# Up projection with high and low activations in one 512-column operand; layer 0 started from a transposed x

## The chip, the core and the metric

The kernel runs on one core of a Trainium2 chip. Its engines, each with an instruction stream of its own: TensorE (PE, matmuls; PEld is its weight load), VectorE (DVE), ScalarE (ACT), GpSimd (POOL) and SyncE (SP, which here issues the transfers). Matmul results go to PSUM, all other tiles lie in SBUF. The metric is device time in microseconds (us), the median of several runs. Three runs of the kernel before gave 849.73, 849.77 and 851.79 us.

## The reference

Two decoder layers on 256 positions of 1024 channels, batch 1, all float32. In the names of the reference, a layer is:

```python
h = rmsnorm(x, norm_mix_pre)
proj = h @ w_in                       # 1024 -> 7168, split into the branches:
q, k, v, g_ret, sc_b, sc_c, sc_x, cf_a, cf_b, gate_logits = split(proj)
y_ret = (silu(g_ret) * head_groupnorm(retention(rotary(q), rotary(k), v))) @ w_ret_out
y_sc  = (sc_b * causal_dwconv(sc_c * sc_x, 3 taps)) @ w_sc_out
y_cf  = silu(layernorm(causal_dwconv(cf_a * sigmoid(cf_b), 31 taps))) @ w_cf_out
x = x + rmsnorm((sum of sigmoid(gate) * y over the three branches) @ w_o, norm_mix_post)
h = rmsnorm(x, norm_ffn_pre)
gate, val = split(causal_dwconv(h @ w_up, 3 taps))          # 1024 -> 2 x 2816
x = x + rmsnorm((silu(gate) * val) @ w_down, norm_ffn_post)
```

rmsnorm divides each row by the root of its mean square and multiplies by a gain per channel.

## The kernel before

**Precision.** Every matmul operand is held as a high part (rounded to TensorE's reduced float32 form) and a low part (what is left). A product takes three matmuls: high x high, high x low, low x high. The weights are split on the chip: ScalarE copies the raw unit into the high tile (L106), VectorE subtracts for the low tile (L107). Activations are split in the same way by `split` (L173 to L175).

**Weights.** All weights are packed on the host into units of 128 x 1024 float32 (512 KB), 142 per layer, in the order of their use. `Weights` (L66) loads a unit into one of four raw buffers (L79, on SP's queue), splits it into one of nine high/low pairs, and runs up to eight units ahead of the one in use (`pump`, L88). Units 0 to 11 of a layer and some later ones are split in two halves of 512 columns (`HALF`). A raw buffer can be loaded again once its low part is made.

**Two forms of projection.** In `xs_unit` (L304) the activation (128 channels by 128 positions) is stationary and 512 weight columns move: Q with K, V, the retention gate G, and the branch gates. `down_unit` (L315) does the same for the down and output projections. In `ws_block` (L270) the weights are stationary and 256 positions move, so that the result has channels on partitions, as the convolutions want: the conformer and short convolution projections, and the up projection. A block is one unit: for each of 8 slices of 128 channels a high-weight matmul with the high and one with the low activation (L274), then 8 low-weight matmuls (L277), all of 256 columns into the same half of a PSUM tile. `ws_pair` (L295) makes two blocks side by side in one tile. The operand `hT` is four tiles of (2 channel slices) x (high, low) x 256 positions.

**The start.** SP loads x of the first 128 rows, the identity, the gain (broadcast to all partitions), then weight units; x of the other 128 rows comes between. `prenorm` (L232) sums the squares on ScalarE, takes the power on GpSimd (L212) and multiplies on VectorE (L237). `to_hT` (L241) transposes on TensorE and splits into `hT`. Twelve matmuls on zeros (L200) run meanwhile. Layer 0 then computes Q and K for both row halves, with V between them, `rotary` (L349: four VectorE steps, four transposes, one copy), then the conformer projections (two B and two A pairs), then G, the short convolution, the branch gates and outputs, `w_o`, and the FFN.

**Background work.** Convolution taps, the retention steps and the layer norm are queued in `bgq` and taken off in slots with a budget (`bg`, L283) after projection blocks or units; what is left is forced before the outputs that need it.

**The up projection.** `up(i)` (L705) makes 256 gate and 256 value columns: the gate pair, `conv3` (L691: one ScalarE step and two VectorE taps per block, which read PSUM), Silu, the value pair, `conv3`, product, split. There are 11 pairs; the first two are computed by `fill` with stationary activations while the second norm finishes, and transposed afterwards by `fill_tr` (L754). From pair 3 on, the down matmuls of pair i - 3 follow each `up`. PSUM has eight tiles of 512 columns: four `mm` and four `ac`; in the up loop the `ac` tiles hold the down sums.

## Time and profile before

| what | value |
|---|---|
| median of three runs | 849.77 us (849.73 to 851.79) |
| the profiled execution's own time | 850.51 us |
| its span, first to last instruction | 848.7 us |
| mean granted TensorE clock | 0.994 |
| busy: PE, PEld, DVE, ACT, POOL | 833.5, 740.9, 655.4, 460.9, 17.9 us |
| moved by DMA | 157.02 MB, mean 185 GB/s |

The profile is of one execution. Its times are in microseconds from the start of the span. Rows of the time-ordered view give start and length, engine, line, operation, output<-input tiles, shapes, and in brackets the idle time of that engine before it with what ended the idleness. Rows of groups give line, engine, operation, tiles, shapes and count, then total busy time and the mean in ns, then the idle time before them. Matmuls are pipelined: the distance between the starts of two is what one costs, not its printed length.

### The profile page before, as it was taken

How to read it: one execution, taken by the hardware profiler on the slowest of the kernel's cores; microseconds unless marked ns; L12 is line 12 of the kernel's file. 1: busy time of each engine (PE TensorE's matmuls, PEld its weight loads, DVE VectorE, ACT ScalarE, POOL GpSimd, SP SyncE). 2: the span in 40 equal slices, each digit the busy share in tenths (PEclk: the TensorE clock that was granted, in tenths of full speed). 3: DMA queues.
4: the chain of work that ended last, by engine and by line, in shares of the span. 5: the costliest groups of instructions: out<-in, count | busy, mean ns of one | idle time of the engine just before them, and what ended most of it. 6: DMA issues, size and time to landing. Idle time of an engine off the chain costs nothing.

```text
span 848.7 us, 13172 instructions
## 1 busy us (share of the span) xinstructions
PE 833.5 (98%) x5036; PEld 740.9 (87%) x5036; DVE 655.4 (77%) x1086; ACT 460.9 (54%) x704; POOL 17.9 (2%) x28
## 2 busy tenths in 40 slices
PE   7999999999999999999999999999999999999997
PEld 4798988888879999999879899888887899999995
DVE  5889999775777976766695999996677698767652
ACT  5664464465666655455665435444666565555541
POOL 0000100000010000000010000000000000000000
PEclk8999999999999999999999999999999999999999
DMA  7885456655665565556566544566555555566511
GB/s 258 309 276 171 149 180 192 201 174 194 200 198 176 180 193 191 180 179 196 172 220 202 175 149 151 193 196 195 182 181 193 175 186 187 179 192 195 179 49 50
DMA packets 43695, 157.02 MB, mean 185 GB/s; under 512 B 4848, under 2 KB 5104, under 8 KB 43632
## 3 DMA queue, kind: packets, MB, share of 16 engines
q1 hardware_dynamic: 43632, 156.18, 57.2%
q8 instruction: 39, 0.64, 0.3%
q14 instruction: 24, 0.20, 0.1%
HBM read 155.12 MB, written 1.05 MB: 184 GB/s over the span
## 4 chain that ended last, share of the span: by engine, by line
PE 92%; DVE 2%; DMA 2%; issue 1%; ACT 1%; POOL 1%; SPq 0%; DVEq 0%; POOLq 0%; ACTq 0%
PE mm L274 25%; PE mm L277 13%; PE mm L309 8%; PE mm L311 8%; PE mm L310 8%; PE ac L320 5%; PE ac L322 5%; PE ac L324 5%; PE ac L311 4%; PE ac L309 4%; PE ac L310 4%; DMA raw<-w_dram 2%; DVE wlo L107 1%; PE mm L245 1%; POOL tn L212 1%
## 5 line engine op out<-in xcount | busy, mean ns | idle before, releaser
L106 ACT ACTIVATE whi<-raw 128x1024 fp32r<-128x1024 f32 (+1 forms) x320 | 296.5, 940 | 277.8 <-PE mm L274 109.2
L107 DVE TENSOR_TENSOR wlo<-raw,whi 128x1024 fp32r<-128x1024 f32 (+1 forms) x320 | 341.0, 1074 | 129.9 <-ACT whi L106 126.3
L274 PE MATMUL mm<-act,whi 128*128 128x256 f32 x1792 | 234.1, 283 | 0.0
L274 PEld LDWEIGHTS mm<-act,whi 128*128 128x128 f32 x1792 | 223.8, 191 | 2.2 <-ACT whi L106 0.7
L277 PE MATMUL mm<-act,wlo 128*128 128x256 f32 x896 | 125.8, 283 | 0.0
L277 PEld LDWEIGHTS mm<-act,wlo 128*128 128x128 f32 x896 | 115.6, 192 | 0.0
L309 PE MATMUL mm<-whi,act 128*128 128x512 f32 x288 | 113.0, 392 | 0.0
L311 PE MATMUL mm<-wlo,act 128*128 128x512 f32 x288 | 112.2, 390 | 0.0
L310 PE MATMUL mm<-whi,act 128*128 128x512 f32 x288 | 112.1, 389 | 0.0
L406 DVE SCALAR_TENSOR_TENSOR big<-big,par 128x229 f32<-128x229 f32 (+27 forms) x240 | 97.0, 462 | 0.0
L698 DVE SCALAR_TENSOR_TENSOR sm<-mm,par,sm 128x254 f32<-128x254 f32 (+1 forms) x176 | 72.7, 474 | 4.0 <-ACT sm L694 3.8
L320 PE MATMUL ac<-whi,act 128*128 128x512 f32 x228 | 71.3, 394 | 0.0
L324 PE MATMUL ac<-whi,act 128*128 128x512 f32 x228 | 70.6, 390 | 0.0
L322 PE MATMUL ac<-wlo,act 128*128 128x512 f32 x228 | 70.4, 390 | 0.0
L311 PEld LDWEIGHTS mm<-wlo,act 128*128 128x128 f32 x288 | 54.1, 188 | 11.4
L310 PEld LDWEIGHTS mm<-whi,act 128*128 128x128 f32 x288 | 54.1, 188 | 10.8
L309 PEld LDWEIGHTS mm<-whi,act 128*128 128x128 f32 x288 | 54.1, 188 | 10.9
L309 PE MATMUL ac<-whi,act 128*128 128x512 f32 x128 | 51.4, 402 | 0.8 <-ACT act L174 0.8
L322 PEld LDWEIGHTS ac<-wlo,act 128*128 128x128 f32 x228 | 42.8, 188 | 9.1
L324 PEld LDWEIGHTS ac<-whi,act 128*128 128x128 f32 x228 | 42.6, 188 | 9.2
L311 PE MATMUL ac<-wlo,act 128*128 128x512 f32 x128 | 50.5, 395 | 0.0
L310 PE MATMUL ac<-whi,act 128*128 128x512 f32 x128 | 50.3, 395 | 0.0
(104 smaller groups left out, 660.0 us busy)
## 6 DMA issues: line engine op xcount, KB each, us to landing
raw<-w_dram SPq DMA_DIRECT2D x284, 512.0 KB, 3.8
gain<-gain_dram SPq DMA_DIRECT2D x7, 512.0 KB, 5.0
xs<-x_dram SPq DMA_DIRECT2D x2, 256.0 KB, 3.2
gain<-gain_dram SPq DMA_DIRECT2D x2, 256.0 KB, 6.0
xs<-x_dram SPq DMA_DIRECT2D x1, 512.0 KB, 10.2
cs<-cst_dram SPq DMA_DIRECT2D x1, 512.0 KB, 6.9
out_dram<-xs SPq DMA_DIRECT2D x1, 512.0 KB, 2.6
out_dram<-xs SPq DMA_DIRECT2D x2, 256.0 KB, 2.0
```

What stands on the lines that cost most here:

```text
L106: self.nc.scalar.activation(out=hi[:, s], in_=r[:, s], func=AF.Copy)
L107: self.nc.vector.tensor_tensor(out=lo[:, s], in0=r[:, s], in1=hi[:, s].bitcast(F32), op=ALU.subtract)
L274: nc.tensor.matmul(o, wh[:, kt * P:(kt + 1) * P], rhs_h(hT, kt, hl), start=(kt == 0 and hl == 0), stop=False)
L277: nc.tensor.matmul(o, wl[:, kt * P:(kt + 1) * P], rhs_h(hT, kt, 0), start=False, stop=(kt == NKT - 1))
L309: nc.tensor.matmul(acc, lhs_h(hT, kt, 0, t), wh[:, s], start=(first and j == 0), stop=False)
L310: nc.tensor.matmul(acc, lhs_h(hT, kt, 1, t), wh[:, s], start=False, stop=False)
L311: nc.tensor.matmul(acc, lhs_h(hT, kt, 0, t), wl[:, s], start=False, stop=(last and j == 1))
L320: nc.tensor.matmul(acc[j], lh[:, tsl], hb(wh, j), start=first, stop=False)
L322: nc.tensor.matmul(acc[j], lh[:, tsl], hb(wl, j), start=False, stop=False)
L324: nc.tensor.matmul(acc[j], ll[:, tsl], hb(wh, j), start=False, stop=last)
L406: nc.vector.scalar_tensor_tensor(out=cc_t[:, b, sh:], in0=glu[:, b, :S - sh], scalar=tap, in1=cc_t[:, b, sh:], op0=ALU.mult, op1=ALU.add)
L698: nc.vector.scalar_tensor_tensor(out=dv[:, b, sh:], in0=pv[:, b, :S - sh], scalar=pp(PW_FF + (blk + b) * KS + 2 - sh), in1=dv[:, b, sh:], ...
```

## The change

Three things change.

In the up projection the high and the low activation of a channel slice, which lie next to each other, become one moving operand of 512 columns for the high weights (`ws_apart`). Products with the high activation land in the left half of a PSUM tile, those with the low one in the right half; the low-weight products, still of 256 columns, are added into the right half. Each block so takes a PSUM tile of its own, and `together` adds the two halves into an SBUF tile, one ScalarE copy and one VectorE add per block. `conv3` then reads SBUF. The transposes of the two filled pairs move to the `ac` tiles, and the value pair of pair 2 is computed ahead of the second filled pair.

Layer 0's Q, V and G are computed from x transposed on the host, times the gain, without the row norm; as the norm is a factor per row, it is applied to the results: in `rotary`, in v's copy, and in G's sigmoid and product. G moves ahead of the conformer projections, also in the order of the packed weights. The row factors are then spread over all partitions by two matmuls of ones with a diagonal, and the normalised operand for the later projections is made from the transposed x (`norm_xT`).

The first half of the first weight unit and the gain column are issued on ScalarE's queue, the first two units in halves; x in its usual form, the cosines and the identity are loaded after the first five units. The Sigmoid table is loaded before anything else on ScalarE's list of functions, and there are 9 warm-up matmuls for 12. The small tiles in SBUF (`sp`) have 10 buffers for 8.

The diff, cut to its core:

```diff
-WARM = 12
+WARM = 9
...
         while self.nd <= min(upto, self.n - 1):
             r = self.rpool.tile([P, 1024], F32, name="raw", tag="raw")
-            self.nc.sync.dma_start(out=r, in_=self.w[self.nd])
+            n = 512 if self.nd < 2 else 1024
+            for c in range(0, 1024, n):
+                eng = self.nc.scalar if self.nd == 0 and c == 0 else self.nc.sync
+                eng.dma_start(out=r[:, c:c + n], in_=self.w[self.nd][:, c:c + n])
             self.raw[self.nd] = r
...
-    sp = ctx.enter_context(tc.tile_pool(name="sp", bufs=8))
+    sp = ctx.enter_context(tc.tile_pool(name="sp", bufs=10))
...
-    nc.sync.dma_start(out=cs[:, :C_COS], in_=cst[:, :C_COS])
-    g_pre0 = gp.tile([P, D], F32, name="gain", tag="gain")
-    for j in range(2):
-        sl = slice(j * 512, (j + 1) * 512)
-        nc.sync.dma_start(out=g_pre0[:, sl], in_=gains[0, 0:1, sl].broadcast_to([P, 512]))
...
+    def load_xT(q):
+        a = xT[q // 2][:, 2 * (q % 2):2 * (q % 2) + 2, :]
+        nc.sync.dma_start(out=a, in_=xt[:, NKT + 512 * q:NKT + 512 * (q + 1)].rearrange("p (a b) -> p a b", b=S))
+
+    def split_xT(q):
+        for j in range(2):
+            kt = 2 * q + j
+            src = xT[kt // 4][:, kt % 4, :]
+            hi, lo = hT0[q][:, j, 0, :], hT0[q][:, j, 1, :]
+            nc.scalar.activation(out=hi, in_=src, func=AF.Identity, scale=gT[:, kt:kt + 1])
+            nc.vector.scalar_tensor_tensor(out=lo, in0=src, scalar=gT[:, kt:kt + 1],
+                                           in1=hi.bitcast(F32), op0=ALU.mult, op1=ALU.subtract)
+
+    load_xT(0)
+    nc.scalar.dma_start(out=gT, in_=xt[:, 0:NKT])
+    W.dma(0)
+    load_xT(1)
+    W.dma(1)
     nc.vector.memset(mhalf, -0.5)
+    ones = const.tile([P, P], F32, name="ones")
+    nc.vector.memset(ones, 1.0)
...
+    def ws_apart(hT, o):
+        i, wh, wl = W.get()
+        for kt in range(NKT):
+            nc.tensor.matmul(o, wh[:, kt * P:(kt + 1) * P],
+                             hT[kt // 2][:, kt % 2, :, :].rearrange("p a b -> p (a b)"),
+                             start=(kt == 0), stop=False)
+        for kt in range(NKT):
+            nc.tensor.matmul(o[:, S:2 * S], wl[:, kt * P:(kt + 1) * P], rhs_h(hT, kt, 0),
+                             start=False, stop=(kt == NKT - 1))
+        W.rel(i)
+
+    def ws_pair_apart(hT):
+        pt = [mm_t(), mm_t()]
+        for b in range(2):
+            ws_apart(hT, pt[b])
+        return pt
+
+    def together(pt):
+        a = sm_t()
+        for b in range(2):
+            ab = a[:, b * S:(b + 1) * S]
+            nc.scalar.activation(out=ab, in_=pt[b][:, S:2 * S], func=AF.Copy)
+            nc.vector.tensor_tensor(out=ab, in0=pt[b][:, 0:S], in1=ab, op=ALU.add)
+        return v2(a)
...
+            def times(out, in0, in1):
+                if rs is None:
+                    nc.vector.tensor_tensor(out=out, in0=in0, in1=in1, op=ALU.mult)
+                else:
+                    nc.vector.scalar_tensor_tensor(out=out, in0=in0, scalar=rs, in1=in1,
+                                                   op0=ALU.mult, op1=ALU.mult)
+
+            times(a.rearrange("p (h d) -> p h d", d=32), ps.rearrange("p (h d) -> p h d", d=32),
+                  cos[t].unsqueeze(1).broadcast_to([P, 16, 32]))
...
+        def ret_g(rs=None):
+            ga = [ac_t(), ac_t()]
+            for k in range(4):
+                u = get_xs(k)
+                for t in range(NT):
+                    xs_unit(u, hT if rs is None else hT0, ga[t], t, k == 0, k == 3)
+                W.rel(u[0])
+                if rs is None:
+                    bg(BG_CF)
+            for t in range(NT):
+                sg = sm_t()
+                if rs is None:
+                    nc.scalar.activation(out=sg, in_=ga[t], func=AF.Sigmoid)
+                    nc.vector.tensor_tensor(out=gs[:, t, :], in0=ga[t], in1=sg, op=ALU.mult)
+                else:
+                    nc.scalar.activation(out=sg, in_=ga[t], func=AF.Sigmoid, scale=rs[t])
+                    nc.vector.scalar_tensor_tensor(out=gs[:, t, :], in0=ga[t], scalar=rs[t], in1=sg,
+                                                   op0=ALU.mult, op1=ALU.mult)
+
...
+        if l == 0:
+            def both(k, acc):
+                u = get_xs(k)
+                for t in range(NT):
+                    xs_unit(u, hT0, acc[t], t, k == 0, k == 3)
+                W.rel(u[0])
+
+            for k in range(4):
+                both(k, qa)
+            rs = [rsq(sum_sq([hb(xs[:, t, :], 0), hb(xs[:, t, :], 1)])) for t in range(NT)]
+            dg = []
             for t in range(NT):
-                xs_unit(u, hT, va[t], t, False, k == 3)
-            W.rel(u[0])
-        for t in range(NT):
-            nc.scalar.activation(out=v_s[:, t, :], in_=va[t], func=AF.Copy)
+                dg.append(sm_t()[:, 0:P])
+                nc.vector.tensor_scalar(out=dg[t], in0=ident, scalar1=rs[t], scalar2=None,
+                                        op0=ALU.mult)
+            both(0, va)
+            rotary(0, qa[0], rs[0])
+            both(1, va)
+            rotary(1, qa[1], rs[1])
+            both(2, va)
+            rows = mm_t()
+            for t in range(NT):
+                nc.tensor.matmul(rows[:, t * P:(t + 1) * P], ones, dg[t], start=True, stop=True)
+            both(3, va)
+            for t in range(NT):
+                nc.scalar.activation(out=v_s[:, t, :], in_=va[t], func=AF.Identity, scale=rs[t])
+
+            def norm_xT(q):
+                xn = sm_t()
+                for j in range(2):
+                    kt = 2 * q + j
+                    nc.vector.scalar_tensor_tensor(out=v2(xn)[:, j, :], in0=xT[kt // 4][:, kt % 4, :],
+                                                   scalar=gT[:, kt:kt + 1], in1=rows[:, 0:S],
+                                                   op0=ALU.mult, op1=ALU.mult)
+                split(v2(xn), hT[q][:, :, 0, :], hT[q][:, :, 1, :])
+
+            for q in range(4):
+                norm_xT(q)
+            ret_g(rs)
+        else:
...
-        ga = [ac_t(), ac_t()]
-        for k in range(4):
-            u = get_xs(k)
-            for t in range(NT):
-                xs_unit(u, hT, ga[t], t, k == 0, k == 3)
-            W.rel(u[0])
-            bg(BG_CF)
-        for t in range(NT):
-            sg = sm_t()
-            nc.scalar.activation(out=sg, in_=ga[t], func=AF.Sigmoid)
-            nc.vector.tensor_tensor(out=gs[:, t, :], in0=ga[t], in1=sg, op=ALU.mult)
+        if l:
+            ret_g()
...
-            pv, dv = v2(ps), v2(dst)
+            pv, dv = ps, v2(dst)
...
-        def up(i, pg=None, pv=None):
-            pg = ws_pair(hT2) if pg is None else pg
+        def up(i, pg=None, pv=None, ga_ps=None):
+            pg = together(ws_pair_apart(hT2) if ga_ps is None else ga_ps) if pg is None else pg
             ga = sm_t()
             conv3(pg, ga, 2 * i)
             gsl = sm_t()
             nc.scalar.activation(out=gsl, in_=ga, func=AF.Silu)
-            pv = ws_pair(hT2) if pv is None else pv
+            pv = together(ws_pair_apart(hT2)) if pv is None else pv
...
         def fill_tr(i):
-            pgv = [mm_t(), mm_t()]
+            pgv = [ac_t(), ac_t()]
...
         up(0, *fill_tr(0))
-        g2 = ws_pair(hT2)
+        g2 = together(ws_pair_apart(hT2))
+        v2_ = together(ws_pair_apart(hT2))
         up(1, *fill_tr(1))
         acc = [[ac_t(), ac_t()] for _ in range(NT)]
         for i in range(NFILL, NPAIR):
-            up(i, *((g2,) if i == NFILL else ()))
+            up(i, *((g2, v2_) if i == NFILL else ()))
...
     hT = new_hT()
-    xg = prenorm(0, g_pre0)
-    to_hT(0, xg, hT)
-    W.pump(1)
-    nc.sync.dma_start(out=xs[:, 1, :], in_=x[P:S, :])
-    W.pump(3)
-    xg = prenorm(1, g_pre0)
-    nc.sync.dma_start(out=cs[:, C_COS:C_DEC], in_=cst[:, C_COS:C_DEC])
+    preload(AF.Sigmoid, mhalf[:, 0:1])
+    for q in range(4):
+        if q > 1:
+            load_xT(q)
+        split_xT(q)
+        W.pump(q)
+    nc.sync.dma_start(out=cs[:, :C_DEC], in_=cst[:, :C_DEC])
+    for t in range(NT):
+        nc.sync.dma_start(out=xs[:, t, :], in_=x[t * P:(t + 1) * P, :])
     W.pump(LOOK)
...
+    if l == 0:
+        xs(win, OFF_G)
     for j in range(2):
         ws(win, OFF_B + 256 * j)
         ws(win, OFF_A + 256 * j)
-    xs(win, OFF_G)
+    if l:
+        xs(win, OFF_G)
...
```

More of the change, by code (lines that the diff above doesn't have):

```diff
@@ L125, in block_kernel @@
 @with_exitstack
-def block_kernel(ctx: ExitStack, tc: tile.TileContext, x, w, gains, par, cst, out):
+def block_kernel(ctx: ExitStack, tc: tile.TileContext, x, xt, w, gains, par, cst, out):
     nc = tc.nc
@@ L347, in get_xs, with rotary @@
             return u
-        def rotary(t, ps):
+        def rotary(t, ps, rs=None):
             a = sm_t()
@@ L382, in layer @@
[L382 to L396 removed]
+        if l == 0:
[8 more added lines that the diff above has]
+            dg = []
+            for t in range(NT):
+                dg.append(sm_t()[:, 0:P])
[24 more added lines that the diff above has]
+        else:
+            uq = [get_xs(k) for k in range(2)]
+            for k in range(2):
+                xs_unit(uq[k], hT, qa[0], 0, k == 0, False)
+            uq += [get_xs(k) for k in range(2, 4)]
+            for k in range(2, 4):
+                xs_unit(uq[k], hT, qa[0], 0, False, k == 3)
+            uv = [get_xs(k) for k in range(2)]
+            for k in range(2):
+                if k == TR1:
+                    to_hT(1, xg1, hT)
+                xs_unit(uv[k], hT, va[0], 0, k == 0, False)
+            for k in range(4):
+                xs_unit(uq[k], hT, qa[1], 1, k == 0, k == 3)
+                W.rel(uq[k][0])
+            rotary(0, qa[0])
+            for k in range(2):
+                xs_unit(uv[k], hT, va[1], 1, k == 0, False)
+                W.rel(uv[k][0])
+            rotary(1, qa[1])
+            for k in range(2, 4):
+                u = get_xs(k)
+                for t in range(NT):
+                    xs_unit(u, hT, va[t], t, False, k == 3)
+                W.rel(u[0])
+            for t in range(NT):
+                nc.scalar.activation(out=v_s[:, t, :], in_=va[t], func=AF.Copy)
@@ L811, in block_kernel @@
     nc.sync.dma_start(out=ps_, in_=par)
+    xg = None
     for l in range(L):
```

44 lines of the change are left out of this document (12 added, 32 removed).

## The prediction

> **What bounds the kernel now.** I read the page's summary and its chain first, then stretches of the span, then the start and one steady piece of the up projection in order of time.
>
> ```profile
> PE 833.5 (98%) x5036; PEld 740.9 (87%) x5036; DVE 655.4 (77%) x1086; ACT 460.9 (54%) x704; POOL 17.9 (2%) x28
> PE 92%; DVE 2%; DMA 2%; issue 1%; ACT 1%; POOL 1%; SPq 0%; DVEq 0%; POOLq 0%; ACTq 0%
> ...
> L274 PE MATMUL mm<-act,whi 128*128 128x256 f32 x1792 | 234.1, 283 | 0.0
> L277 PE MATMUL mm<-act,wlo 128*128 128x256 f32 x896 | 125.8, 283 | 0.0
> ```
>
> TensorE is the bound: 92% of the chain that ended last, and no idle time in front of the two groups that the change rewrites. So time can be taken out in two ways: fewer TensorE cycles, or less time before TensorE is fed. The second is the start, here in order of time (start, length, engine, line, in brackets the idle time before it and its end):
>
> ```profile
> 1.22 4.76 PE L200 MATMUL mm<-warm 128*128 128x512 bf16 x12 [1.22 <-DVE warm L197]
> 3.84 0.63 ACT L219 ACTIVATE junk<-xs 128x512 f32<-128x512 f32 x1 [1.83 <-DMA xs<-x_dram]
> 10.90 1.15 ACT L106 ACTIVATE whi<-raw 128x512 fp32r<-128x512 f32 x2 [5.58 <-DMA raw<-w_dram]
> 11.56 0.69 DVE L107 TENSOR_TENSOR wlo<-raw,whi 128x512 fp32r<-128x512 f32 x1 [1.17 <-ACT whi L106]
> 12.37 0.79 PE L309 MATMUL ac<-whi,act 128*128 128x512 f32 x1 [0.81 <-ACT act L174]
> 12.69 1.28 DVE L107 TENSOR_TENSOR wlo<-raw,whi 128x512 fp32r<-128x512 f32 x2
> 14.28 0.63 PE L310 MATMUL ac<-whi,act 128*128 128x512 f32 x1
> 14.70 0.63 PE L311 MATMUL ac<-wlo,act 128*128 128x512 f32 x1
> 24.22 0.39 PE L310 MATMUL ac<-whi,act 128*128 128x512 f32 x1
> 27.64 0.68 DVE L355 TENSOR_TENSOR sm<-ac,cs 128x512 f32<-128x512 f32 x1
> 33.74 0.39 PE L310 MATMUL ac<-whi,act 128*128 128x512 f32 x1
> 35.40 0.63 PE L365 MATMUL mm<-cs,sm 128*128 128x128 f32 x4 [1.28 <-DVE sm L362]
> 37.49 0.60 PE L365 MATMUL mm<-cs,sm 128*128 128x128 f32 x4
> 39.32 2.08 PE L274 MATMUL mm<-act,whi 128*128 128x256 f32 x16
> ```
>
> The first real matmul is at 12.37, because the first weight unit landed only at 10.9, behind x, the identity and the broadcast gain on one queue. It then runs at half speed (14.28 to 14.70 is 0.42 us; later, 24.22 to 33.74 holds 42 intervals, 0.2267 each). The first rotary's transposes come at 35.40 after 1.28 us of idle TensorE, and the conformer branch, the first work after Q and V, begins at 39.32. The first rotary step stands at 27.64 between weight splits though the code has it behind them: each engine's stream is ordered by a planner that lets ready work pass, not strictly as written.
>
> ```profile
> 0.00:40.00 40.00, 32.89 (x138) 24.00 (x139) 26.47 (x49) 23.48 (x46) 1.31 (x6) 0.91 0.84 287
> 13.00:35.00 22.00, 21.12 (x91) 16.81 (x90) 19.64 (x37) 15.13 (x32) 0.55 (x1) 0.94 0.86 288
> 263.00:290.00 27.00, 27.00 (x218) 26.55 (x217) 24.89 (x42) 18.17 (x30) 0.00 (x0) 1.00 0.59 184
> 310.00:420.00 110.00, 110.00 (x757) 102.85 (x756) 74.49 (x105) 59.05 (x83) 0.00 (x0) 1.00 0.59 192
> ```
>
> These are stretches: width, then busy us of PE, PEld, DVE, ACT and POOL, granted clock, DMA share, GB/s. From 13 to 35 VectorE is busy 19.64 of 22 us (89%), so the start is nearly a VectorE bound too: it makes the low parts of the weights. In the steady up projection (310 to 420) it is busy 68%, ScalarE 54%; at the entry to it (263 to 290) VectorE is busy 92%.
>
> **The up projection.** One steady pair, its first block and the down matmuls behind it:
>
> ```profile
> 309.79 2.08 PE L274 MATMUL mm<-act,whi 128*128 128x256 f32 x16
> 311.70 1.12 PE L277 MATMUL mm<-act,wlo 128*128 128x256 f32 x8
> 321.30 0.63 PE L320 MATMUL ac<-whi,act 128*128 128x512 f32 x2
> 326.77 1.48 PE L274 MATMUL mm<-act,whi 128*128 128x256 f32 x11
> ```
>
> From 309.79 to 321.30 four blocks of 24 matmuls are issued: 11.51 / 96 = 0.120 us per 256-column matmul. From 321.30 to 326.77 stand 24 matmuls of 512 columns: 0.228 each. Two of 256 thus cost 0.240, one of 512 costs 0.228, and 0.012 is saved each time. A block has 16 high-weight matmuls, which become 8: 8 x 0.012 = 0.097 us. Nine pairs per layer (2 to 10) have gate and value with two blocks each: 36 blocks, 72 in both layers, and 72 x 0.097 = **7.0 us**. With the 0.2267 of the start in place of 0.228 it would be 7.7; that is the upper end.
>
> What is added: per block a ScalarE copy of 256 columns out of PSUM and a VectorE add that brings the two halves together.
>
> ```profile
> L175 DVE TENSOR_TENSOR act<-mm,act 128x256 fp32r<-128x256 f32 x48 | 19.7, 418 | 3.2 <-ACT act L174 3.0
> L174 ACT ACTIVATE act<-mm 128x256 fp32r<-128x256 f32 x48 | 17.7, 379 | 22.3 <-PE mm L245 17.6 <-DVE act L175 4.1
> L698 DVE SCALAR_TENSOR_TENSOR sm<-mm,par,sm 128x255 f32<-128x255 f32 x88 | 38.2, 476 | 4.0 <-ACT sm L694 3.8
> ```
>
> By these, a pair (16.98 us now, 309.79 to 326.77) gets 4 x 0.42 = 1.7 us more of VectorE and 4 x 0.38 = 1.5 more of ScalarE. In 110 us lie 6.5 pairs: VectorE goes from 74.5 to 85.4 of some 107 us (80%), ScalarE from 59 to 69 (64%). TensorE's work covers both, so I cost them at nothing; if the cover were gone the price would be the 1.6 us of one evacuation (two copies, two adds) per gate or value. The convolution behind it reads SBUF instead of PSUM; I take the same 0.476. A gate or value now holds two of the four PSUM tiles instead of one, so the next gate must wait until this gate is evacuated; between them lie the value's two blocks (5.6 us) and the down matmuls (5.5 us), 11 us of cover against 1.6.
>
> At the entry, VectorE has 27 - 24.9 = 2.1 us free in 27, and four gates or values there add 4 x 0.84 = 3.4 while 0.8 us of TensorE time goes: 2 us too much per layer. The weights, split up to eight units (some 22 us) ahead, take that up; without them it is up to 2 us twice. Taking the value of pair 2 ahead of the second filled pair changes no amount of work.
>
> **The start of layer 0.** Removed: both input norms, their gain broadcast, 16 transposes and eight splits. Added: 1 MB of transposed x (x itself, 1 MB, comes later and no longer gates), eight splits of it with the gain as a scale, the row factor applied in the rotary, v and gate steps, two matmuls that spread it, and four pieces of normalised operand. The gate projection G (48 matmuls) moves ahead of the conformer: the old time to compare is 39.3 + 48 x 0.2267 = 50.2 us.
>
> *First matmul.* A 256 KB transfer issued first landed at 3.84; two high splits of 256 columns (0.38 each) give 4.6, the first half of the weights 0.6 more, 5.2, its low part 0.7 more, 5.9. The page has no load on the ScalarE queue; I take it like SP's, and its table load (1.28 us) as done by then. The nine warm-up matmuls at 0.43 end near 5.2, so no gap of the old length (5.98 to 8.09) precedes the real ones.
>
> *TensorE's floor.* 6.0 + 144 x 0.2267 + 8 rotary transposes (1.0) + the two spreading matmuls (0.3) = 39.9 us.
>
> *VectorE's bound.* Its means:
>
> ```profile
> L107 DVE TENSOR_TENSOR wlo<-raw,whi 128x1024 fp32r<-128x1024 f32 x232 | 283.4, 1222 | 124.2 <-ACT whi L106 122.2
> L175 DVE TENSOR_TENSOR act<-sm,act 128x512 fp32r<-128x512 f32 x30 | 20.5, 684 | 0.7 <-ACT act L174 0.7
> L237 DVE SCALAR_TENSOR_TENSOR big<-xs,tn,gain 128x512 f32<-128x512 f32 x16 | 11.5, 749 | 6.6 <-DMA gain<-gain_dram 3.3 <-POOL tn L212 3.3
> L359 DVE TENSOR_TENSOR sm<-ac,cs 128x256 f32<-128x256 f32 x8 | 3.1, 415 | 0.0
> L362 DVE TENSOR_TENSOR sm<-sm 128x512 f32<-128x512 f32 x4 | 2.8, 690 | 0.1
> ```
>
> Before the conformer can begin it must do 8 x splits (3.3 us), the low parts of units 0 to 11 in halves (12 x 1.28 = 15.4) and 12 to 15 whole (4.9), two rotaries now with a scalar (0.75 + 2 x 0.42 + 0.69, twice: 4.5), the normalised operand (8 x 0.42 + 4 x 0.68 = 6.1) and small pieces (0.8, my estimate from the 0.21 of a one-column step): 35.0 us. At the old share of 89% that is 39.2 us, from 4.2 on: 43.4. This lies above TensorE's floor, so I take it: 50.2 - 43.4 = **6.8 us** gained. The floor would give 10.3. The other end is the first rival.
>
> Weights do not run short before that: a raw buffer comes free when its low part is made (the queue's waits name it), now from 6.6 instead of 12.9, which leaves room for the extra megabyte.
>
> ```profile
> SPq L79 <- DVE wlo L107: 29.5, 16, 6.4
> ```
>
> *Behind it.* G no longer carries four background slots, so eight convolution taps move to later slots. Walking the slots by their budgets, the list is empty at the first of the eight gate units of branch 2 before the change and at the third after it, five units ahead of the forced emptying: nothing on the path. Layer 1's start stays.
>
> **Sum.** 850.5 (the profiled execution, span 848.7 and 1.8 around it) - 7.0 - 6.8 = 836.7. That execution lies 0.7 above the median of 849.77, so I forecast **836.0 us**.
>
> **The rivals.**
>
> *TensorE held at the first rotary (0.16).* If the stream keeps the written order, the transposes stand behind 60 matmuls (reached near 19.7), and the rotary behind unit 12's low part: 4.2 + (3.3 + 15.4 + 1.2 + 0.8) / 0.89 + 2.3 = 29.7. Then 84 matmuls and the rest follow (19.0 + 1.3) and the second rotary costs 0.8 more: 50.8, no gain, 843.4 us. For it: the 1.28 us before 35.40 is this wait. Against it: 83 matmuls had been passed ahead of it there, not the 60 that the code has.
>
> *VectorE overflows at the entry (0.07).* 2 us in each layer: 840.
>
> *The 0.012 us belong to something else than the count (0.05).* Then the up projection gives about nothing beyond a fifth: 850.5 - 6.8 - 1.4 - 0.7 = 841.6. The rows speak against it: 256 / 2.4 and 512 / 2.4 would leave 13 and 15 ns over in both widths, at one frequency. The Trainium skill's "TensorE: Matmul & The Clock Gate" (section "Back-to-back issue gap") puts an isolated warm gap at N / 2.4 + 2.5 ns, by which a dropped matmul would save 2.5 ns and the up projection 72 x 8 x 2.5 ns = 1.4 us, an estimate from that page; the rows here show 120 and 228 ns against its 109 and 216, so the trace does not agree.
>
> *Neither part does what it says (0.06).* Both of the above at once: 849.
>
> *Evacuation throttles the up projection: slower (0.08).* If the next gate waits for the evacuation of the last one on every pair, because VectorE runs its queue in order behind weight splits and convolutions, the price is up to 1.6 us for each of 36 gates and values, 58 us; at half that, 850 - 14 + 29 = 865. It decides from 13.8 / 36 = 0.38 us of wait per gate or value. Against it stand the 11 us of cover and VectorE's 80%.
>
> **Chances and range.** The forecast has 0.58, its own range 832 to 840 (floor to 10.3 at one end; a start gain of 3 at the other). To leave out no more than 0.2 I take 831 to 845, which holds the first rival. A difference under 0.3% (2.5 us) is one that a measurement of this kernel can't tell from none. Faster: 0.58 + 0.16 + 0.07 + 0.05 = 0.86; the same 0.06; slower 0.08.
>
> **What would show it.** In the changed profile: an up block in 2.78 us instead of 2.88, a pair in 16.6 instead of 16.98, no idle time before the 512-column matmuls; the first real matmul near 5.5 at full clock; the conformer's first block near 43, with VectorE and not a DMA named before it; the rotary transposes later than 60 matmuls. I am wrong if TensorE shows gaps inside the up pairs, if the first weights land after 7, or if TensorE stands for several us before the rotary's transposes.

## The result, and the profile after

The changed kernel takes **835.53 us** in the median of four runs (835.33 to 835.61); the kernel before, run beside it, takes 850.03 (849.73 to 851.79). The ratio is 0.9825 with a 95% interval of 0.981 to 0.984: 14.5 us faster. The forecast was 836.0 in a range of 831 to 845. The profiled execution took 835.61 us with a span of 833.8 and a mean granted clock of 0.998.

The summary page of the kernel after: busy time with share of the span and count, then the shares of the chain that ended last.

```profile
PE 822.5 (99%) x4445; PEld 707.9 (85%) x4445; DVE 684.3 (82%) x1169; ACT 483.7 (58%) x780; POOL 18.8 (2%) x28
PE 96%; DVE 1%; issue 1%; POOL 1%; DMA 1%; ACT 0%; DVEq 0%; POOLq 0%; ACTq 0%
```

TensorE still bounds the kernel, more than before: its share of the chain rose from 92% to 96%. Its trace holds 591 matmuls fewer, 576 of them by the merging in the up projection. VectorE does 29 us more and ScalarE 23 us more, and neither gained in the chain.

The groups of the same kernel: line, engine, operation, tiles, shapes, count, then busy time and mean ns, then the idle time before them.

```profile
L303 PE MATMUL mm<-act,whi 128*128 128x512 f32 x576 | 144.2, 392 | 0.0
...
L798 DVE SCALAR_TENSOR_TENSOR sm<-sm,par 128x255 f32<-128x255 f32 x72 | 32.7, 482 | 9.0 <-ACT sm L794 9.0
L322 DVE TENSOR_TENSOR sm<-mm,sm 128x256 f32<-128x256 f32 x72 | 28.2, 418 | 1.0 <-ACT sm L321 1.0
L321 ACT ACTIVATE sm<-mm 128x256 f32<-128x256 f32 x72 | 24.4, 369 | 0.0
```

No idle time stands before the wide matmuls (L303). The added copy (L321, 369 ns) and add (L322, 418 ns) cost what similar rows had said, and the convolution that now reads SBUF (L798) takes 482 ns where 476 was the row before.

One steady pair of the up projection after, in order of time:

```profile
283.05 1.98 PE L303 MATMUL mm<-act,whi 128*128 128x512 f32 x8
...
294.19 0.63 PE L364 MATMUL ac<-whi,act 128*128 128x512 f32 x2
...
299.66 0.62 PE L303 MATMUL mm<-act,whi 128*128 128x512 f32 x2
```

Four blocks from 283.05 to 294.19 are 2.785 us each, and the pair from 283.05 to 299.66 is 16.61 (before: 2.88 and 16.98).

The start after, several engines in one order of time:

```profile
1.36 3.82 PE L219 MATMUL mm<-warm 128*128 128x512 bf16 x9 [1.36 <-DVE warm L216]
3.85 0.91 ACT L203 ACTIVATE act<-big,gT 128x256 fp32r<-128x256 f32 x2 [0.70 <-DMA gT<-xt_dram]
5.59 1.15 ACT L109 ACTIVATE whi<-raw 128x512 fp32r<-128x512 f32 x2 [0.83 <-DMA raw<-w_dram]
6.27 0.50 PE L353 MATMUL ac<-whi,act 128*128 128x512 f32 x1 [1.10 <-ACT whi L109]
6.61 0.39 PE L354 MATMUL ac<-whi,act 128*128 128x512 f32 x1
26.82 0.60 PE L415 MATMUL mm<-cs,sm 128*128 128x128 f32 x4
...
38.52 0.69 DVE L178 TENSOR_TENSOR act<-sm,act 128x512 fp32r<-128x512 f32 x1
...
40.54 3.03 PE L293 MATMUL mm<-act,whi 128*128 128x256 f32 x24
43.50 1.13 PE L549 MATMUL ac<-big 64*128 64x256 f32 x4
44.21 1.29 DVE L178 TENSOR_TENSOR act<-sm,act 128x512 fp32r<-128x512 f32 x2
```

The first real matmul is at 6.27 instead of 12.37 and runs near full speed at once. The first rotary's transposes (26.82) come without idle time. The conformer begins at 40.54, with Q, V **and** G done; the old time to compare is 50.2.

Stretches of the kernel after: width, busy us of PE, PEld, DVE, ACT and POOL with counts, granted clock, DMA share, GB/s.

```profile
13.00:35.00 22.00, 22.00 (x104) 18.18 (x103) 16.98 (x34) 14.87 (x30) 1.11 (x2) 1.00 0.91 337
254.00:281.00 27.00, 27.00 (x156) 23.73 (x155) 25.28 (x44) 18.93 (x34) 0.00 (x0) 1.00 0.54 181
283.00:400.00 117.00, 117.00 (x620) 100.94 (x620) 97.70 (x156) 75.61 (x124) 0.00 (x0) 1.00 0.58 189
```

TensorE is busy throughout all three. VectorE stands at 94% at the entry of the up projection (254 to 281) and at 84% in its steady part.

To say where the time came from, the same points of the program are read in both traces: the transposes of the first filled pair in layer 0, those of layer 1's first norm, those of the filled pair in layer 1, the last matmul, and the last stores. Before:

```profile
262.57 1.04 PE L758 MATMUL mm<-cs,sm 128*128 128x128 f32 x8
427.39 1.32 PE L245 MATMUL mm<-cs,big 128*128 128x128 f32 x8 [0.60 <-DVE big L237]
677.00 1.04 PE L758 MATMUL mm<-cs,sm 128*128 128x128 f32 x8
842.20 0.39 PE L332 MATMUL ac<-whi,act 128*128 128x512 f32 x1
845.12 1.00 SPq L798 DMA_DIRECT2D out_dram<-xs  x2
```

After:

```profile
253.50 1.03 PE L858 MATMUL ac<-cs,sm 128*128 128x128 f32 x8
415.14 1.07 PE L264 MATMUL mm<-cs,big 128*128 128x128 f32 x6 [0.68 <-DVE big L256]
664.78 1.04 PE L858 MATMUL ac<-cs,sm 128*128 128x128 f32 x8
826.73 0.39 PE L376 MATMUL ac<-whi,act 128*128 128x512 f32 x1
829.66 0.99 SPq L899 DMA_DIRECT2D out_dram<-xs  x2
```

| stretch | before | after | gain |
|---|---|---|---|
| start of the span to the filled pair of layer 0 | 262.57 | 253.50 | 9.07 |
| from there to layer 1's first transposes (up projection, layer 0) | 164.82 | 161.64 | 3.18 |
| from there to the filled pair of layer 1 | 249.61 | 249.64 | -0.03 |
| from there to the last matmul (up projection, layer 1) | 165.20 | 161.95 | 3.25 |
| last matmul to the issue of the last stores | 2.92 | 2.93 | -0.01 |
| from there to the end of the span | 3.58 | 4.14 | -0.56 |
| span | 848.7 | 833.8 | 14.9 |

So the start gave 9.1 us, the up projection 6.4, and the end after the last stores cost 0.6.

### The profile page after: what moved, and what is told of

Its sections match the earlier page's. It is cut to its first block, busy times and chain, and to the rows that moved or that the text cites. A ratio compares the mean times of both kernels' runs of the same rounds, so it can differ in the third digit from the quotient of the medians.

```text
span 833.8 us, 12168 instructions
## 1 busy us (share of the span) xinstructions
PE 822.5 (99%) x4445; PEld 707.9 (85%) x4445; DVE 684.3 (82%) x1169; ACT 483.7 (58%) x780; POOL 18.8 (2%) x28
## 4 chain that ended last, share of the span: by engine, by line
PE 96%; DVE 1%; issue 1%; POOL 1%; DMA 1%; ACT 0%; DVEq 0%; POOLq 0%; ACTq 0%
PE mm L303 16%; PE mm L293 9%; PE mm L307 8%; PE mm L355 8%; PE mm L354 8%; PE mm L353 8%; PE ac L364 5%; PE ac L366 5%; PE ac L368 5%; PE mm L296 5%; PE ac L353 4%; PE ac L355 4%; PE ac L354 4%; PE mm L264 1%; DVE wlo L110 1%
## 5 line engine op out<-in xcount | busy, mean ns | idle before, releaser
L303 PE MATMUL mm<-act,whi 128*128 128x512 f32 x576 | 144.2, 392 | 0.0
L303 PEld LDWEIGHTS mm<-act,whi 128*128 128x128 f32 x576 | 104.4, 189 | 19.2
L515 DVE SCALAR_TENSOR_TENSOR big<-big,par 128x229 f32<-128x229 f32 (+29 forms) x240 | 97.5, 465 | 0.0
L293 PE MATMUL mm<-act,whi 128*128 128x256 f32 x640 | 84.4, 284 | 0.0
L307 PEld LDWEIGHTS mm<-act,wlo 128*128 128x128 f32 x576 | 78.6, 190 | 5.6
L293 PEld LDWEIGHTS mm<-act,whi 128*128 128x128 f32 x640 | 79.8, 192 | 1.4 <-DVE act L178 0.3
L307 PE MATMUL mm<-act,wlo 128*128 128x256 f32 x576 | 80.3, 282 | 0.0
L798 DVE SCALAR_TENSOR_TENSOR sm<-sm,par 128x255 f32<-128x255 f32 (+1 forms) x144 | 63.4, 481 | 9.9 <-ACT sm L794 9.0
L364 PE MATMUL ac<-whi,act 128*128 128x512 f32 x228 | 71.3, 394 | 0.0
L368 PE MATMUL ac<-whi,act 128*128 128x512 f32 x228 | 70.5, 391 | 0.0
L366 PE MATMUL ac<-wlo,act 128*128 128x512 f32 x228 | 70.5, 390 | 0.0
L353 PE MATMUL ac<-whi,act 128*128 128x512 f32 x128 | 50.7, 396 | 1.1 <-ACT whi L109 1.1
```

Of the source, the lines that this page charges most:

```text
L293: nc.tensor.matmul(o, wh[:, kt * P:(kt + 1) * P], rhs_h(hT, kt, hl), start=(kt == 0 and hl == 0), stop=False)
L303: nc.tensor.matmul(o, wh[:, kt * P:(kt + 1) * P], hT[kt // 2][:, kt % 2, :, :].rearrange("p a b -> p (a b)"), start=(kt == 0), stop=False)
L307: nc.tensor.matmul(o[:, S:2 * S], wl[:, kt * P:(kt + 1) * P], rhs_h(hT, kt, 0), start=False, stop=(kt == NKT - 1))
L353: nc.tensor.matmul(acc, lhs_h(hT, kt, 0, t), wh[:, s], start=(first and j == 0), stop=False)
L364: nc.tensor.matmul(acc[j], lh[:, tsl], hb(wh, j), start=first, stop=False)
L366: nc.tensor.matmul(acc[j], lh[:, tsl], hb(wl, j), start=False, stop=False)
```

## The experiments

All runs are compared with the kernel before on the same chip (850.25 us in the median for the first four experiments; 850.29 for G put back, one queue for the weights, three warm-ups and the wide projections; 849.77 for the three with all loads on SP; 849.95 for the last). The kernel before is thus the common measure of the groups; its medians differ by 0.5 us at most.

**The up part alone**, put into the kernel before:

```diff
-            pg = ws_pair(hT2) if pg is None else pg
+            pg = together(ws_pair_apart(hT2) if ga_ps is None else ga_ps) if pg is None else pg
...
-            pv = ws_pair(hT2) if pv is None else pv
+            pv = together(ws_pair_apart(hT2)) if pv is None else pv
...
-        g2 = ws_pair(hT2)
+        g2 = together(ws_pair_apart(hT2))
+        v2_ = together(ws_pair_apart(hT2))
```

> The kernel before with the up projection's part alone (one 512-column operand, a PSUM tile for each block, the halves added afterwards, 10 small tiles); its start is the old one. Theory: the two parts add up, and this one is worth what the landmarks of the two traces show behind the first filled pair, 3.2 us in each layer: 6.5 us less than before, 843.5, a block in 2.79 us. Rival: part of the 6.5 came from the earlier start (a VectorE that is less behind when the up projection begins); then this run gains less than 5 us. Rival by 2.5 ns for each matmul saved: 1.4 us.

Measured: 843.51 us (842.91 to 843.95), ratio 0.9916 (0.99 to 0.9932): 6.7 us faster. In its trace the two up projections, from the filled pair's transposes on, take 161.68 and 161.96 us against 164.82 and 165.20. The term of 7.0 holds but for 0.3 to 0.6.

**The start alone**: the changed kernel with the old up projection (the edit above undone).

> The changed kernel with the old up projection (two 256-column matmuls, one PSUM tile for a pair, no additions afterwards). Theory: the start alone is worth 9.1 us, 841.0, and with the run of the up part alone the two sum up to the whole change within 1 us. Rival (the parts need each other): the sum of the two gains is off the whole by more than 2 us.

Measured: 842.29 us (841.52 to 843.27), ratio 0.9904 (0.9884 to 0.9925): 8.0 us faster, 1.2 more than the term of 6.8. The parts add up: 6.7 + 8.0 = 14.7, against 14.5 for the whole change. The trace of this run gained 9.1 us up to its last matmul (842.20 to 833.10), but its span only 8.5 (848.7 to 840.2): its end, too, is 0.6 us longer.

**Is it the number of matmuls or the layout?** The 512-column matmul is issued as two of 256 into the same halves; copy, add and tiles stay:

```diff
-            nc.tensor.matmul(o, wh[:, kt * P:(kt + 1) * P],
-                             hT[kt // 2][:, kt % 2, :, :].rearrange("p a b -> p (a b)"),
-                             start=(kt == 0), stop=False)
+            for hl in range(2):
+                nc.tensor.matmul(o[:, hl * S:(hl + 1) * S], wh[:, kt * P:(kt + 1) * P],
+                                 rhs_h(hT, kt, hl), start=(kt == 0 and hl == 0), stop=False)
```

> The changed kernel, but each 512-column matmul of the up projection is made as two of 256 columns again, into the same two halves of the same tile; copies and additions stay. Theory (the gain is a fixed cost for each matmul): blocks go back to 2.88 us and the up projection's whole gain is lost: 6.5 us more than the changed kernel, 842. Rival (the gain comes from the layout: weights loaded with less conflict, separate tiles): the time stays within 2 us of the changed kernel.

Measured: 842.99 us (842.05 to 843.59), ratio 0.9909 (0.9892 to 0.9926), 7.5 us above the changed kernel. Its steady pair, in order of time:

```profile
301.81 2.08 PE L304 MATMUL mm<-act,whi 128*128 128x256 f32 x16
...
318.79 2.08 PE L304 MATMUL mm<-act,whi 128*128 128x256 f32 x16
```

318.79 - 301.81 = 16.98, the pair of the kernel before to the hundredth. The whole gain of the up projection goes with the count of matmuls. This kernel lies 0.7 us over the start alone (842.29), which has neither copies nor adds, and the runs of the two overlap, so the copies and adds cost nothing that can be told from none.

**Does the evacuation need its cover?** The up projection is confined to two PSUM tiles of its own, and two are left to all others, so that a value must wait for its gate's evacuation:

```diff
-    mmp = ctx.enter_context(tc.tile_pool(name="mmp", bufs=4, space=PS))
+    mmp = ctx.enter_context(tc.tile_pool(name="mmp", bufs=2, space=PS))
...
+    def mu_t():
+        return mmp.tile([P, 512], F32, name="mu", tag="mu")
...
-        pt = [mm_t(), mm_t()]
+        pt = [mu_t(), mu_t()]
```

> The changed kernel with the up projection's blocks confined to two PSUM tiles of their own, and two left to all other users of that pool. So each gate or value must wait for the evacuation of the one before it, which takes away the 11 us of cover. Read in the up projection alone. Theory: each of 36 gates and values then waits for the first block's evacuation, with matmuls of the down projection between only once per pair: a pair takes 16.6 + 1 to 3 us, 18 to 54 us in all. Rival (evacuation is quick enough to hide behind the second block): a pair stays under 17 us.

Measured: 849.57 us in one run. The steady pair of this kernel:

```profile
323.09 1.98 PE L306 MATMUL mu<-act,whi 128*128 128x512 f32 x8
...
339.70 1.98 PE L306 MATMUL mu<-act,whi 128*128 128x512 f32 x8
```

339.70 - 323.09 = 16.61: the pair is as short as with four tiles. The theory (18 to 54 us lost in the pairs) fell. The reading is that while the second block of a gate or value is computed (2.8 us), the first one's copy and add (0.37 + 0.42) are done, so that the next gate or value finds its first tile free. The 11 us of cover that the prediction counted were not needed. The 14 us over the changed kernel lie elsewhere, by the traces' distances: 4.3 us up to the filled pair of layer 0 (257.75), 2.5 and 2.6 in the two up projections outside the steady pairs, 4.6 between them. Of the 4.3, 1.8 are there before the conformer begins (42.36 for 40.54), in an execution whose first nine real matmuls ran at half speed (see the last section). For the rest the two tiles that serve everything else are the likely cause; that is argued, not tested.

**What is G's move worth?** In the changed kernel, G goes back behind the conformer in layer 0, weights and code:

```diff
-            ret_g(rs)
...
-        if l:
-            ret_g()
+        ret_g()
...
-    if l == 0:
-        xs(win, OFF_G)
```

> The changed kernel with the gate projection G of layer 0 back behind the conformer projections, made from the normalised operand as in layer 1, and its weights in the old place. Q and V still start from the transposed x. The conformer then follows Q and V near 30 us, while its operand was complete only near 45.5 us in the changed kernel. Theory (G ahead is the cover for the normalised operand): TensorE waits before or within the conformer, the operand being ready near 38 to 40 us, so 6 to 9 us are lost: 842 to 845. Rival (the planner finds other work, or VectorE makes the operand earlier when asked earlier): less than 3 us lost, below 838.5.

Measured: 848.15 us (847.06 to 848.39, ten runs), ratio 0.9974 (0.9964 to 0.9984): 12.6 us above the changed kernel, more than the 6 to 9 expected. TensorE's waits from 26 to 46, and the stretches (columns as above):

```profile
PE mm L293 <- ACT act L177: 3.0, 2, 1.6
PE mm L415 <- DVE sm L412: 2.8, 1, 2.8
```

```profile
28.00:33.00 5.00, 2.71 (x14) 1.89 (x12) 4.24 (x8) 3.35 (x7) 0.00 (x0) 1.00 0.95 355
33.00:36.00 3.00, 1.19 (x8) 0.91 (x8) 1.55 (x4) 1.76 (x3) 0.00 (x0) 0.74 1.03 419
36.00:39.00 3.00, 2.31 (x9) 2.02 (x10) 3.00 (x4) 2.58 (x4) 0.00 (x0) 0.50 0.64 216
39.00:42.00 3.00, 1.58 (x7) 1.28 (x7) 3.00 (x5) 1.95 (x3) 0.00 (x0) 0.50 0.75 270
42.00:45.00 3.00, 3.00 (x13) 2.65 (x13) 3.00 (x7) 1.57 (x3) 0.00 (x0) 0.55 0.94 314
```

Idle TensorE makes 2.29 + 1.81 + 0.69 + 1.42 = 6.2 us here. On top of it the granted clock falls to half: busy time times the missing share is 0.3 + 1.2 + 0.8 + 1.4 = 3.6. The first ten matmuls of this execution also ran at half speed (6.07 to 10.50, 4.43 us instead of 2.27), 2.2 more. Together 12.0, and the retention's matmuls of scores with values are indeed 11.7 us later than in the changed kernel (87.19 against 75.52). The 2.2 belong to the slow start that the last section treats, not to G's place. So in this order the prediction's VectorE bound does hold TensorE up (VectorE is busy without a gap from 36 to 45, and the waits name the second rotary, L412, and the making of the normalised operand, L177), and the fallen clock adds 3.6 us to the 6.2 of idleness. Without G ahead, the new start is 4.6 us worse than no new start at all (848.15 against 843.51 for the up part alone), and still 2.4 worse if the 2.2 are taken off.

**The second queue.** The first half of the first weight unit is issued by SP like the rest (only the gain's 4 KB stay on ScalarE's queue):

```diff
-                eng = self.nc.scalar if self.nd == 0 and c == 0 else self.nc.sync
+                eng = self.nc.sync
```

> The changed kernel with the first half of the first weight unit issued on SP's queue like the other loads; the gain column stays on ScalarE's. SP then issues one more transfer of 0.42 us ahead of the first weights. Theory: the first weights land up to 0.4 us later, the first real matmul is at 6.3 to 6.7 us, and the total changes by less than 0.5 us, which the comparison can't tell from none. Rival (the two queues matter): the first matmul comes over 1 us later and the total rises by as much.

Measured: 836.2 us (835.88 to 837.01), ratio 0.9839 (0.9825 to 0.9854): no difference from the change. The start of this run:

```profile
1.36 3.43 PE L219 MATMUL mm<-warm 128*128 128x512 bf16 x9 [1.36 <-DVE warm L216]
5.76 0.50 PE L353 MATMUL ac<-whi,act 128*128 128x512 f32 x1 [0.97 <-ACT whi L109]
```

Its first real matmul is *earlier*, at 5.76 instead of 6.27, against the 6.3 to 6.7 expected. In the changed kernel the half unit on ScalarE's queue takes 4.40 us from 1.17 on. The 0.5 us is not kept: the conformer's first block is at 40.91 here, at 40.54 in the changed kernel. The Trainium skill's "DMA: Bandwidth & Descriptors" (section "Issuing engines are not separate DMA queues") says that transfers issued from different engines run interleaved on the same 16 DMA engines and that only issue time is saved. The runs agree in so far as the second queue brought nothing earlier; here the half unit took 3.5 us from SP's queue, 0.9 less.

**All loads on one queue**, the gain too:

```diff
-    nc.scalar.dma_start(out=gT, in_=xt[:, 0:NKT])
+    nc.sync.dma_start(out=gT, in_=xt[:, 0:NKT])
```

> The changed kernel with all loads on SP's queue: the gain column and the first half of the first weight unit too. In every run so far whose kernel issues a load from ScalarE the span ends 7.1 us after the last matmul, in the two that issue none 6.5, though the steps up to the last store are alike. Theory (a second queue in use costs its own closing at the end): the end is 6.5 us again, 0.57 less; with a first matmul near 5.8 to 6.3 the time is 0.3 to 1 us under the changed kernel, 834.5 to 835.2. Rival (the longer end comes from something else in the new start): the end stays at 7.1.

Measured: 836.74 us (836.37 to 837.62), ratio 0.9849 (0.9836 to 0.9863). The theory that a second queue lengthens the end fell: from the last matmul to the end of the span this run takes 6.9 us (828.87 to 835.8), like the changed kernel's 7.1 and not the 6.5 of the kernel before and of the up part alone.

**Fewer warm-up matmuls**, three instead of nine:

```diff
-WARM = 9
+WARM = 3
```

> The changed kernel with 3 warm-up matmuls for 9. They end near 2.6 us and TensorE then stands until 6.3. Theory: the first real matmuls run at half clock for about 3 us, as in the kernel before (0.42 us each against 0.227), and 1.3 to 1.6 us are lost, 837. Rival (the start is bound by the splits and not by TensorE): less than 0.5 us lost though the clock is low.

Measured: 837.52 us (836.62 to 838.15), ratio 0.9852 (0.9838 to 0.9867), 2.0 over the changed kernel in the medians, where 1.3 to 1.6 was expected. All four runs lie above those of the changed kernel, but the profiled one, the fastest, by only 1.0, so the direction is clear and the size is not. Its first real matmuls:

```profile
6.03 0.79 PE L353 MATMUL ac<-whi,act 128*128 128x512 f32 x1 [3.21 <-ACT whi L109]
7.05 0.63 PE L353 MATMUL ac<-whi,act 128*128 128x512 f32 x1
7.47 0.63 PE L354 MATMUL ac<-whi,act 128*128 128x512 f32 x1
...
9.66 0.40 PE L353 MATMUL ac<-whi,act 128*128 128x512 f32 x1
```

They stand 0.42 us apart until about 9.2, where the changed kernel has 0.23.

**The same rewrite for the other projections.** The conformer's and short convolution's projections get wide matmuls too:

```diff
-        pt = mm_t()
+        pt = [mm_t(), mm_t()]
...
-        ws_block(hT, pt[:, 0:S])
+        ws_apart(hT, pt[0])
...
-        return pt
+        return together(pt).rearrange("p a b -> p (a b)")
```

> The changed kernel with the conformer and short convolution projections made in the same way as the up projection: 40 more blocks with 512-column matmuls and their additions. Theory: TensorE saves 40 x 0.09 = 3.6 us, 832; VectorE gets 10 x 0.75 us more per layer in a stretch where it is 98% busy (75 to 120 us). Rival (VectorE has no room there): the additions delay the weights or the PSUM tiles and the time is the same or worse, 835 to 845.

Measured: 835.35 us (835.04 to 836.34), ratio 0.983 (0.9815 to 0.9844): as the changed kernel. Yet the projections gained: from the conformer's first block to the output projection this trace has 164.15 us in layer 0 and 174.25 in layer 1, the changed kernel 165.38 and 175.66. That is 2.6 us of the 3.6 expected; 2.1 of it were lost at the start:

```profile
1.36 4.02 PE L219 MATMUL mm<-warm 128*128 128x512 bf16 x9 [1.36 <-DVE warm L216]
6.43 0.80 PE L353 MATMUL ac<-whi,act 128*128 128x512 f32 x1 [1.05 <-ACT whi L109]
...
7.44 0.63 PE L353 MATMUL ac<-whi,act 128*128 128x512 f32 x1
7.87 0.63 PE L354 MATMUL ac<-whi,act 128*128 128x512 f32 x1
...
10.83 0.40 PE L354 MATMUL ac<-whi,act 128*128 128x512 f32 x1
```

The start's code is that of the changed kernel, but here the matmuls run at half speed until about 10.4, which costs 1.9 us, and the conformer begins at 42.63 instead of 40.54.

**Wide projections with all loads on SP**, then **in layer 1 only**: the edits above combined.

> The run with the conformer and short convolution projections made in 512-column form, with all loads on SP's queue. Theory: where all projections were wide, the parts of the span from the conformer to the output projection were 1.2 to 1.4 us shorter in each layer, and a later conformer start, 42.6 for 40.5, that varies by about 1 us from run to run, hid it; then this run is 2 to 3 us under the changed kernel, 832.5 to 833.5. Rival (the later start is caused by the additions in layer 0, through the planner's order): it again starts the conformer above 42 and is within 1 us of the changed kernel.

> As the run before, but in layer 1 only; layer 0 keeps the two 256-column matmuls there. Theory: the conformer of layer 0 starts near 40.5 as in the changed kernel, layer 1 gains 1.4 us, the end 0.57: 833.5. Rival: no difference from the run with wide projections in both layers, which is then better by what layer 0 gains.

Measured: 835.46 us (835.19 to 836.64), ratio 0.9836 (0.9822 to 0.9849), and 836.06 (835.69 to 836.85), ratio 0.9843 (0.9829 to 0.9856). Both missed what was expected: they are 1.3 and 0.7 us under the one-queue kernel of the same group (836.74), intervals overlapping. The conformer began at 41.78 and 42.02 in these, over a microsecond later than in the changed kernel. The second has no additions in layer 0's conformer, so they are not the cause. The kernel with all loads on SP and no wide projection at all begins its conformer later still:

```profile
42.51 3.03 PE L293 MATMUL mm<-act,whi 128*128 128x256 f32 x24
```

In all three of these kernels TensorE waits for VectorE before the second rotary's transposes (1.0 us in this one, 0.2 and 0.4 in the other two), which it does not in the changed kernel. So the late begin comes without wide projections too. Whether all loads on SP cause it is not shown: there is one trace for each, and the kernel with the split matmul, whose loads are those of the changed kernel, also began its conformer late, at 41.61. The projections themselves gained less than hoped: 0.2 us in layer 0 where all are wide (165.21 for 165.38), as TensorE waited 1.0 us there for an addition, and 0.8 instead of 1.4 in layer 1 where only that layer is wide (174.84 for 175.66).

**Wide projections with twelve warm-ups**, to keep TensorE busy until the weights are there:

```diff
-WARM = 9
+WARM = 12
```

> The run with the conformer and short convolution projections in 512-column form (loads as in the changed kernel), with 12 warm-up matmuls for 9. In that run the first ten real matmuls were 0.43 us apart, half speed, and the conformer began at 42.6 for 40.5. Theory (nine warm-up matmuls end too early to be sure of the full clock, and the wide projections themselves are worth about 2.5 us): the first real matmul comes at 6.3 to 6.6 at full speed, the conformer near 40.7, the time is 2 us under the changed kernel, 833.3 to 833.8. Rival (the later conformer start comes with the additions): at full speed from the first matmul the conformer still starts above 42 and the time stays within 0.7 us of the changed kernel.

Measured: **832.95 us** (832.74 to 834.08, five runs) against 849.95 of the kernel before: ratio 0.9807 (0.9794 to 0.982). Its five runs all lie under the four of the changed kernel, by 2.6 us in the median; the two ratios' intervals (the changed kernel's begins at 0.981) overlap by 0.001. Against nine warm-ups with the same projections it is 2.4 us less, or 2.1 when each is set against the kernel before on its chip. It is the best version here. Its start:

```profile
1.36 5.30 PE L219 MATMUL mm<-warm 128*128 128x512 bf16 x12 [1.36 <-DVE warm L216]
6.28 0.81 PE L353 MATMUL ac<-whi,act 128*128 128x512 f32 x1
6.88 0.45 PE L354 MATMUL ac<-whi,act 128*128 128x512 f32 x1
7.18 0.40 PE L355 MATMUL ac<-wlo,act 128*128 128x512 f32 x1
```

No idle time stands before the real matmuls, and from the third on they are at full speed. The twelve warm-ups themselves all ran at half speed: three more of them took 5.30 - 4.02 = 1.28 us more, 0.43 each. The conformer begins at 40.81, 1.8 us before the run with nine warm-ups, and the filled pair of layer 0 is reached at 252.11 instead of 254.37; behind that the two traces are equal (578.9 us both).

## Why the prediction was right, point by point

The forecast of 836.0 met 835.53, and part of that is luck: the gain of the start was costed by a limit that did not act, and the sizes of three terms were off in opposite directions: it had -7.0 and -6.8 (13.8), the traces show -6.4, -9.1 and +0.6 (14.9); in medians of the parts alone, -6.7 and -8.0 (14.7). Of the rest, the forecast took 0.7 off for the profiled execution, which lies 0.5 above the median of 850.03.

- **Up projection: right, a little large.** A block takes 2.785 us where 2.78 was forecast, a pair 16.61 where 16.6 was. Splitting the wide matmul again brings the pair back to 16.98, which settles the rival that the 0.012 us belong to something other than the count. Eighteen steady pairs times 0.37 make 6.7, which is what the part alone gave in the median; the traces' distances hold 6.4. Where the remaining 0.3 went is not settled. The isolated gap that the Trainium skill's "TensorE: Matmul & The Clock Gate" gives (section "Back-to-back issue gap") would have made 1.4 us of it; the runs rule that out for this stream.
- **The evacuation costs nothing: right, and safer than argued.** The cover counted was 11 us between two gates. With only two tiles the steady pair is still 16.61, so one block suffices. The slower rival (865) was never near.
- **Entry overflow: did not come.** From 254 to 281 VectorE is busy 25.28 of 27 us and TensorE 27.00; the up projections gain the same in both layers (3.18 and 3.25).
- **First real matmul: 6.27, forecast 5.9 to 6.0.** The step took ScalarE's queue like SP's, and let ScalarE begin on the weights at 4.6. The half unit landed only at 5.57; that the step also waited 0.7 us for the low part, which the first matmul does not read, hid most of this. With the half unit on SP's queue the first matmul came at 5.76.
- **VectorE's bound on the start: the step that failed.** The forecast took the time when the normalised operand is complete (43.4) as the time when TensorE can go on with the conformer. The operand was complete only at 45.5 (the row at 44.21 above), 2.1 us *later* than forecast, and still TensorE had begun the conformer at 40.54 and did not wait. The second of the operand's four quarters was there at 39.21 (the row at 38.52). With these two quarters TensorE ran the first slices of three blocks (24 matmuls in one row at 40.54, 8 for each block), and then pulled retention scores forward (43.50). The planner's habit of letting ready work pass, which the prediction had read in the old trace, was used there only against the first rival. So the start ran close to TensorE's floor: 10.3 us was the gain by that floor, 0.3 is lost by the late first matmul, 0.3 more up to the conformer's begin (50.2 - 40.54 = 9.7), and 0.6 behind it.
- **How sure the 9.1 is.** The up-part kernel has the old start, and its trace reaches the filled pair at 261.33, 1.2 us before that of the kernel before. Against that execution the new start gained 7.8 us there, and in the median the start alone gave 8.0. The gain at the start is 7.8 to 9.1 by these, above 6.8 either way.
- **G ahead of the conformer.** The prediction counted it only as 48 matmuls to be added to the old time. The run with G put back, worse than no new start at all, shows that it is the condition for any gain from the start: while VectorE still makes the normalised operand, G feeds TensorE with work that doesn't need it.
- **First rival (TensorE held at the first rotary): fell.** The transposes are at 26.82 with no idle time before them, and TensorE is busy 22.00 of 22 us from 13 to 35.
- **Moved convolution taps: nothing on the path, as forecast.** Between the up projections both kernels take 249.6 us.
- **Not foreseen:** the end behind the last stores is 0.56 us longer.

## What to carry to other kernels

Where TensorE is busy throughout, two matmuls with the same weights and neighbouring columns are worth merging for the matmul that disappears (0.012 us each here), and a copy and an add per block are a fair price as long as one block of TensorE time covers them (in one run with the wide conformer projections it did not, once, for 1.0 us). A bound worked out for a helper engine is a bound on the consumer only if the consumer has nothing else that is ready: list what needs none of the late operand, and put it ahead, as G is here. When the first transfers come sooner, bridge the time until they land with warm-up matmuls to the end, and read TensorE's rate from the distance of its starts.

## What the runs showed of the hardware that was not expected

**Nine warm-ups are not enough to have the clock up.** They take 3.4 to 4.0 us. In the runs with nine where they took 3.41 to 3.82, the first real matmuls stood 0.23 apart; in four runs (two tiles, G back, wide projections, wide projections in layer 1) all nine took 4.02, and the real ones began at half speed, in three of them for nine or ten matmuls. In the one trace of the new start with twelve no gap was left, and only the first two real matmuls were slow. The code up to the first matmul differs in these ten at most in the queue of a load, and slow starts came with both, so what differs is when the clock rises. The Trainium skill's "TensorE: Matmul & The Clock Gate" (Part 1, on the clock gate) says that the clock follows activity in a free-running window of about 3.4 us, counted in time and not in matmuls, and that the number of slow ones varies from run to run; the rows here agree with that (from none to ten slow real matmuls behind nine warm-ups). With one trace for each kernel it is not shown how often each of them starts slowly, nor that twelve always suffice.

**The granted-clock column does not show this slow start.** The stretch of the kernel with wide projections and nine warm-ups in which its matmuls stand 0.43 us apart:

```profile
7.00:8.00 1.00, 1.00 (x4) 0.80 (x3) 1.00 (x3) 1.00 (x3) 0.00 (x0) 1.00 1.07 422
```

Four matmuls in a microsecond are half speed, but the clock is given as 1.00. Later in a run the column does show it (0.50 with G put back).

**Short gaps bring the clock down.** With G put back, no wait of TensorE is longer than 2.8 us, yet the granted clock was half from 36 to 42, behind a stretch (28 to 36) in which TensorE was busy 3.9 of 8 us.

**The end.** Every run with the new start and a trace read at its end needs 6.9 to 7.1 us from the last matmul to the end of the span, the two with the old start 6.5. The second queue is not the cause alone, since the kernel with all loads on SP has 6.9. What it is stays open.
